# Two layers of a hybrid decoder, one step: masks, norms and state loads of the matrix-memory layer arranged in another way

## The chip, the cores and the metric

The kernel runs on one core of one Trainium2 chip. The metric is the device time of one execution in microseconds (us), from launch to end; the median of several runs is given. "The profiled execution" is one execution taken by the hardware profiler, and its span is the stretch from its first to its last recorded instruction. TensorE (PE) multiplies matrices, its weight loads (PEld) run beside it; VectorE (DVE), ScalarE (ACT) and GpSimd (POOL) work element by element; SyncE (SP) issues most of the transfers. PSUM is the memory that TensorE writes to; a bank of it is 512 float32 columns here.

## The reference

A trunk of two layers is applied to a prompt of 256 tokens and to 8 samples of 8 tokens each, 320 tokens of width 1024 in all, with the same weights. Layer 0 mixes tokens by a chunked spatial gate, layer 1 by a matrix memory (mLSTM) with 8 heads, keys of 128 and values of 256; a gated feed-forward layer with a short convolution follows each. The change touches the memory layer alone. Cut to what matters:

```python
p = rmsnorm(x, g) @ w_in                       # q, k, v, o and the gates i, f of 8 heads
qk = silu(causal_dwconv(p_qk, conv_buf, conv_w, conv_b))
# per head, in chunks, exact recurrence:
sc  = einsum('td,sd->ts', q, k) * exp(D - m_t)
num = w_inter * (q @ C) + sc @ v
den = w_inter * (q @ n) + sum(sc)
h   = num / max(|den|, exp(-m_t))
C_new = decay * C + (k * g).T @ v
n_new = decay * n + sum(k * g)
# group norm of each head's row, then the output gate
hn = (h - mean(h)) * rsqrt(var(h) + EPS) * gn_g
y  = (sigmoid(o) * hn) @ w_out
```

Returned are, beside the activations, the new states C, n and m for the prompt and for each of the 8 samples.

## The kernel before, in words

The activations lie transposed in SBUF, 8 tiles of 128 features by 320 tokens. Weights pass through once, in blocks of 128 by 1024 (`raw`, 4 buffers, loaded by SP's queue in a fixed order). Float32 accuracy is had from reduced-precision passes: each `raw` is cast to a high part `wh` by ScalarE (line 129), and VectorE subtracts to a low part `wl` (line 130); activations are split likewise (`xh`, `xl`). One block is 24 matmuls into a PSUM tile `pm`: high by high, high by low, low by high for each of 8 k-tiles (`chunk`, `block`). The order of TensorE's instructions is written out by hand and pinned; the order on VectorE, ScalarE, GpSimd and SP is made by a scheduler from data, buffers and the order of the source. PSUM tiles come from two pools, `psm` (3 banks, the blocks) and `psa` (5 banks, everything else); which of the 5 banks a tile gets is settled when the program is built, and a matmul then waits until that bank's last readers are through.

The memory layer, `layer_b`, lies at some 430 to 735 us of the profile.

`gates` comes first. A block `pg` gives the two gates of all heads. `norm_cols` then sums the squares of each token by matmuls against ones (three tiles of tokens, two passes each, into `pc`), and GpSimd raises the mean to the power -1/2 (`rc`, a token per partition). With `twice=True` the third tile is a copy `acc2` in which each sample token stands twice (line 210), because the sample rows of the values are kept doubled. The first q block `p0` follows on TensorE, then `norm_row` turns `rc` into a row for all partitions (`dg`, `pb`, `rb`). After that come the exponents and running maxima of the gates, five further blocks, and the transposes `pt` that give them per token (`colsT`). When `gates` ends, the pool of its rows closes and the pool `hb` opens.

Each head h then goes through two q and k blocks (`qk_epi`), two v blocks (`v_epi`), and two o blocks (`o_epi`), and between them, in TensorE's order:

- `scores`: the mask rows `pMb`, the scores `psc`, exponentials `w` by ScalarE, `Pf` = scores times `w`, split into `Ph` and `Pl`; the sample part goes to `Ps` in two disjoint halves, the first of which, `Pr`, is made by VectorE (line 690);
- `k_nat`: the keys transposed back (`pk`), scaled and split for the prompt (`kgh`, `kgl`), and for the samples `kz`, which is the key times one mask minus `kr`, the key times another (lines 721 and 722, VectorE);
- `finish(h - 1)`: the normalised rows `hn` transposed (`phn`), gated (`y_b`) and split (`yhb`, `ylb`, lines 839 and 840);
- `v_nat`: the values transposed back (`pv`), scaled by `rc` and split (`vh`, `vl`, lines 705 and 706);
- `hand_over`: 16 matmuls of the queries with the states C into `num` (`inter`), products `pcs` of keys and values of the samples, four tiles (`state_sample`), and the first two updates of C (`state_out`, line 762);
- in the next head `close` (the other two updates, the rest of the numerators, the prompt's state `pCp`) and `stats`: means and variances of the numerators (`mv`), the denominators `dn` and their maximum `rd`, the scale `sl` and the offset `nb`, and `hn` by ScalarE (line 801).

`state_in(h)` asks for the four states of a head (`C0`); head 0's is called after `gates`, because its tiles come from `hb`. Of the output weights, some blocks are worked early, in heads 4 to 6. The last head has a tail of its own. The first loop pass (h = 1) also holds the second half of head 0, so its order differs: `hand_over(0)` follows the first k block, `stats(0)` the second v block.

Of the kernel before, what the change touches and what calls it, by code (L numbers as in the profile page):

```python
# [10 lines left out]
F32 = mybir.dt.float32  # L11
F32R = mybir.dt.float32r
AF = mybir.ActivationFunctionType
# [3 lines left out]
P = 128  # L17
EPS = 1e-6
TP = 256
NB, NS = 8, 8  # L20
T = TP + NB * NS
D = 1024
# [3 lines left out]
NH = 8  # L26
# [11 lines left out]
class Net:  # L38
# [150 lines left out]
    @staticmethod  # L189
    def spread(x):  # L190

        return x.rearrange("p (g d s) -> p g d s", g=4, d=2)
# [8 lines left out]

    def norm_cols(self, parts=None, twice=False):

        nc = self.nc
        parts = parts or [self.acc]
        pc = self.psa.tile([P, 512], F32, tag="pa", name="pc")
        pv = pc[:, 0:6].rearrange("p (t e) -> p t e", e=2)
        if twice:
            acc2 = self.tp.tile([P, P], F32, tag="acc2", name="acc2", bufs=1)
            nc.vector.tensor_copy(self.spread(acc2), self.twice(self.acc[:, TP:]))  # L210
        for t in range(3):
            for i, a in enumerate(parts):
                a_t = acc2 if twice and t == 2 else self.tokens(a, t)
                self.mm(pv[:, t, :], a_t, self.ones[:, :2], i == 0, i == len(parts) - 1)
        rc = self.tp.tile([P, 3], F32, tag="rc", name="rc", bufs=2)
        ms = self.tp.tile([P, 3], F32, tag="ms", name="ms", bufs=2)
        nc.vector.tensor_scalar(ms, pv[:, :, 0], 1.0 / D, EPS, op0=MULT, op1=ADD)
        nc.gpsimd.tensor_tensor(rc, ms, self.mhalf.to_broadcast([P, 3]), op=ALU.pow)
        self.rc, self.rc_twice = rc, twice

    def norm_row(self):

        nc = self.nc
        dg = self.tp.tile([P, T], F32, tag="sq", name="dg", bufs=2)
        pb = self.psa.tile([P, 512], F32, tag="pa", name="pb")
        for t in range(2):
            nc.vector.tensor_scalar(dg[:, t * P:(t + 1) * P], self.ident, self.rc[:, t:t + 1], None, op0=MULT)
        if self.rc_twice:
            nc.vector.tensor_scalar(dg[:, TP:].rearrange("p (g s) -> p g s", g=4), self.spread(self.ident)[:, :, 0, :],
                                    self.rc[:, 2:3], None, op0=MULT)  # L230
        else:
            nc.vector.tensor_scalar(dg[:, TP:], self.ident[:, 64:], self.rc[:, 2:3], None, op0=MULT)
        self.mm(pb[:, :T], self.ones, dg, True, True)
        rb = self.tp.tile([P, T], F32, tag="rb", name="rb", bufs=1)
        nc.scalar.copy(rb, pb[:, :T])
        self.rb = rb
# [261 lines left out]
    def layer_b(self):  # L498
# [5 lines left out]
        with ExitStack() as ctx:  # L504
# [4 lines left out]
            nS = lp.tile([P, NH, NB], F32, name="nS")  # L509
            nP = lp.tile([P, NH], F32, name="nP")  # L510
            gnh = lp.tile([P, 16], F32, name="gnh")
            colsT = lp.tile([P, 3, 96], F32, name="cols")
            X = lp.tile([P, 392], F32R, name="X")
            sel = lp.tile([P, NH, P], F32R, name="sel")
            mk = lp.tile([P, NB + 5], F32, name="mk")
            mxb = lp.tile([P, 64], F32, name="mxb")
            gm = lp.tile([P, 4, NH], F32, name="gm")
            mo = lp.tile([8, 9], F32, name="mo")
            mkr = lp.tile([P, NB], F32R, name="mkr")
            pads = []  # L520
# [11 lines left out]
            def gates(rp):  # L532
# [34 lines left out]
                nc.vector.tensor_tensor(gr, pg[:64, :T], gr, op=ADD)  # L567
                self.norm_cols(twice=True)
                p0 = self.block(KD, self.x_rhs)
                self.norm_row()  # L570
                nc.vector.tensor_tensor(zi, gr[:40], self.rb[:40, :], op=MULT)
                qk_epi(0, 0, p0)
                nc.vector.tensor_scalar(zi, zi, bif[:, 0:1], None, op0=ADD)
                nc.vector.scalar_tensor_tensor(az, z, -1.0, z, op0=MULT, op1=MAX)
# [84 lines left out]
            def scores(h):  # L659
# [8 lines left out]
                mm(sc[:, 384:448], s["ks"], q[:, TP:T], True, True)  # L668
                dec = hp.tile([P, NB], F32, tag="dec", name="dec", bufs=2)
                nc.vector.tensor_copy(dec, pb[:, 384:392])  # L670
                Qd = Qz.rearrange("p (g i r) -> p g i r", g=4, i=2)[:, :, :, :NS]
# [8 lines left out]
                for o in (0, TP):  # L680
# [8 lines left out]

                nc.vector.tensor_scalar(Pr, Pf[:, 384:], mk[:, NB:NB + 1], None, op0=MULT)  # L690
                nc.vector.tensor_tensor(spread(Ps)[:, :, 0, :], Pf[:, 384:].rearrange("p (g s) -> p g s", g=4),
                                        Pr.bitcast(F32).rearrange("p (g s) -> p g s", g=4), op=SUB)
                s["P"] = (Ph, Pl, dec)

            def v_nat(h):
                s = S[h]
                pv = [self.psa.tile([P, 512], F32, tag="pa", name="pv") for _ in range(2)]
                dsts = [pv[t // 2][:, (t % 2) * DV:] for t in range(3)]
                for t in range(3):
                    for e in range(2):  # L700
                        self.tr(dsts[t][:, e * P:(e + 1) * P], s["vT"][e][:, t * P:(t + 1) * P], self.ident)
                for t in (2, 0, 1):
                    dst = dsts[t]
                    sc = self.rc[:, t:t + 1]
                    nc.scalar.activation(vh[:, t, :DV], dst[:, :DV], AF.Copy, scale=sc)
                    nc.vector.scalar_tensor_tensor(vl[:, t, :DV], dst[:, :DV], sc, vh[:, t, :DV].bitcast(F32), op0=MULT, op1=SUB)

            def k_nat(h):
# [6 lines left out]
                kgl = hp.tile([P, 2, P], F32R, tag="kgl", name="kgl", bufs=1)  # L715
                kr = hp.tile([P, 2, P], F32R, tag="kr", name="kr", bufs=1)
                kz = hp.tile([P, 2, P], F32R, tag="kz", name="kz", bufs=1)
                src = pk[:, 2 * P:3 * P]

                for i in range(2):  # L720
                    nc.vector.tensor_scalar(kr[:, i, :], src, gm[:, 2 + i, h:h + 1], None, op0=MULT)
                    nc.vector.scalar_tensor_tensor(kz[:, i, :], src, gm[:, i, h:h + 1], kr[:, i, :].bitcast(F32), op0=MULT, op1=SUB)
                for t in range(2):
# [6 lines left out]
            def state_in(h):  # L730
                S[h]["C"] = []
                for i in range(4):
                    C0 = hp.tile([P, 2, CW], F32, tag="C0", name="C0", bufs=8)
                    nc.sync.dma_start(C0, I["C0"][h, :, 2 * i:2 * i + 2, :])
                    S[h]["C"].append(C0)

# [43 lines left out]
            def stats(h):  # L780
# [8 lines left out]
                nc.vector.tensor_tensor(rd, dn, colsT[:, :, 64 + h], op=MAX)  # L789
                nc.vector.reciprocal(rd, rd)  # L790
                t1 = hp.tile([P, 3], F32, tag="t1", name="t1", bufs=1)
                nc.vector.tensor_tensor(t1, mv[:, :, 1], rd, op=MULT)
                nc.vector.tensor_tensor(t1, t1, rd, op=MULT)
                nc.vector.tensor_scalar(t1, t1, EPS, None, op0=ADD)
                sl = hp.tile([P, 3], F32, tag="sl", name="sl", bufs=1)
                nc.gpsimd.tensor_tensor(sl, t1, self.mhalf.to_broadcast([P, 3]), op=ALU.pow)
                nc.vector.tensor_tensor(sl, sl, rd, op=MULT)
                nb = hp.tile([P, 3], F32, tag="nb", name="nb", bufs=1)
# [4 lines left out]
            def state_prompt(h):  # L803
                s = S[h]
                kgh, kgl, kz = s["kg"]
                dec = s["P"][2]
                pc = self.psa.tile([P, 512], F32, tag="pa", name="pCp")
                for t in range(2):
                    mm3(pc[:, :CW], kgh[:, t, :], kgl[:, t, :], vh[:, t, :], vl[:, t, :], t == 0, t == 1)
                for i in range(2):  # L810
                    mm(pc[:, 264:272], kz[:, i, :], mkr, i == 0, i == 1)
                Cp = hp.tile([P, DV], F32, tag="Cp", name="Cp", bufs=1)
                nc.scalar.copy(Cp, pc[:, :DV])
                nc.sync.dma_start(O["Cp"][h], Cp)
                nc.scalar.copy(nP[:, h:h + 1], pc[:, DV:DV + 1])
                nc.vector.tensor_tensor(nS[:, h, :], n0[:, h, :], dec, op=MULT)
                nc.vector.tensor_tensor(nS[:, h, :], nS[:, h, :], pc[:, 264:272], op=ADD)

# [71 lines left out]

            state_in(0)
            scores(0)
# [60 lines left out]
            begin(2)  # L953
            nc.sync.dma_start(O["nP"], nP)
            nc.sync.dma_start(O["nS"], nS)
# [59 lines left out]
def _lay_out(i):  # L1015
# [56 lines left out]
    for h in range(NH):  # L1072
# [3 lines left out]
    tok = s // 32 * 16 + s % 16  # L1076
    low, odd = s // 16 % 2, s // 8 % 2
    a["blk"] = np.concatenate([tok[:, None] // NS == np.arange(NB)[None, :], np.stack(
        [low, 1 - odd, odd, (1 - odd) * low, odd * low], axis=1)], axis=1).astype(f)
    a["mxb"] = np.where((tok[:, None] // NS == q[None, :] // NS) & (tok[:, None] <= q[None, :]), f(-1e30), f(1e4))  # L1080
# [27 lines left out]
```

## Time and profile before

| what | value |
|---|---|
| time, median of 3 runs | 977.2 us (976.13, 977.2, 979.38) |
| the profiled execution: its time | 977.89 us |
| its span | 975.8 us |
| TensorE busy | 957.5 us |
| VectorE, ScalarE, GpSimd busy | 686.7, 484.6, 71.9 us |
| data moved | 154.73 MB, mean 159 GB/s |

A row of a timeline gives start and duration in us, the engine, the line of the code, the operation, output and inputs by the program's names, size, and how many instructions of the kind are taken together; in brackets stands how long the engine had been idle before, and after an arrow what ended that. A row of the waits gives for an engine's line who released it, then the sum, how often and the longest. A group's row gives busy time and the mean of one in ns. The clock is the share of full speed that TensorE was granted.

### The profile page before, as it was taken

Reading aid. Unit: us, or ns where it says so; the run is one execution under the profiler, and the core shown is the slowest. Engines: PE = TensorE matmul, PEld = TensorE weight load, DVE = VectorE, ACT = ScalarE, POOL = GpSimd, SP = SyncE. Lnnn points to the kernel's source line nnn. Section 1 sums busy time; section 2 is a strip of 40 time slices with the busy share of each in tenths; the row PEclk is TensorE's granted clock in tenths of the full one; section 3 lists DMA queues with packets and bytes.
Section 4 is the critical chain, followed back from the end, with each engine's and each line's share of the span. In section 5 each row is a group of like instructions: output and inputs, shape, how many; then the busy total and the mean of one; then the engine's idle time right before and its main releaser. Section 6 shows DMA issues by size and latency. Waiting matters only on the chain. (4 is left out here: it accounts for less than half of the span.)

```text
span 975.8 us, 17507 instructions
## 1 busy us (share of the span) xinstructions
PE 957.5 (98%) x6703; PEld 941.0 (96%) x6703; DVE 686.7 (70%) x1344; ACT 484.6 (50%) x846; POOL 71.9 (7%) x238
## 2 busy tenths in 40 slices
PE   9999999999999999999989999999999999999996
PEld 8999999999999999999889999999899999999996
DVE  6647985577777764548988887787787777775442
ACT  6437444445554543347456665464565455544332
POOL 0200000010000000012200110011001000000000
PEclk9999999999999999999999999999999999999999
DMA  8534434434444445553854556545273444444441
GB/s 283 193 119 159 140 133 155 152 133 149 151 152 151 148 147 152 150 190 101 279 188 156 189 174 221 170 160 164 73 239 137 152 152 151 152 146 149 147 129 54
DMA packets 55944, 154.73 MB, mean 159 GB/s; under 512 B 6758, under 2 KB 17638, under 8 KB 55862
## 3 DMA queue, kind: packets, MB, share of 16 engines
q1 hardware_dynamic: 55862, 153.62, 47.4%
q8 instruction: 53, 0.87, 0.4%
q14 instruction: 29, 0.24, 0.1%
HBM read 141.66 MB, written 11.94 MB: 157 GB/s over the span
## 5 line engine op out<-in xcount | busy, mean ns | idle before, releaser
L129 ACT CAST wh<-raw 128x1024 fp32r<-128x1024 f32 (+3 forms) x254 | 257.4, 1014 | 353.0 <-PE pm L47 221.9
L47 PE MATMUL pm<-xh,wh 128*128 128x320 f32 x1344 | 422.7, 315 | 1.2 <-ACT wh L129 1.2
L47 PE MATMUL pm<-xh,wl 128*128 128x320 f32 x1344 | 417.5, 311 | 0.1
L47 PE MATMUL pm<-xl,wh 128*128 128x320 f32 x1344 | 417.0, 310 | 0.0
L130 DVE TENSOR_TENSOR wl<-raw,wh 128x1024 fp32r<-128x1024 f32 (+3 forms) x254 | 300.2, 1182 | 124.5 <-ACT wh L129 122.4
L47 PEld LDWEIGHTS pm<-xh,wh 128*128 128x128 f32 x1344 | 253.9, 189 | 2.4 <-ACT wh L129 1.6
L47 PEld LDWEIGHTS pm<-xh,wl 128*128 128x128 f32 x1344 | 253.6, 189 | 0.7 <-DVE wl L130 0.7
L47 PEld LDWEIGHTS pm<-xl,wh 128*128 128x128 f32 x1344 | 253.9, 189 | 0.2
L47 PE MATMUL pm<-yh_f,wh 128*128 128x320 f32 x352 | 109.1, 310 | 0.0
L47 PE MATMUL pm<-yl_f,wh 128*128 128x320 f32 x352 | 108.6, 309 | 0.0
L47 PE MATMUL pm<-yh_f,wl 128*128 128x320 f32 x352 | 108.6, 309 | 0.0
L47 PEld LDWEIGHTS pm<-yl_f,wh 128*128 128x128 f32 x352 | 66.2, 188 | 0.0
L47 PEld LDWEIGHTS pm<-yh_f,wh 128*128 128x128 f32 x352 | 66.1, 188 | 0.0
L47 PEld LDWEIGHTS pm<-yh_f,wl 128*128 128x128 f32 x352 | 66.1, 188 | 0.0
L420 DVE SCALAR_TENSOR_TENSOR fcv<-fpad,vecs,fcv 128x336 f32<-128x336 f32 x88 | 49.6, 566 | 2.2 <-ACT fcv L418 0.7
L243 DVE TENSOR_TENSOR xT<-pm,xT 128x320 f32<-128x320 f32 x40 | 19.6, 491 | 41.6 <-PE pm L47 41.4
L47 PE MATMUL pm<-yhb,wh 128*128 128x320 f32 x128 | 40.3, 315 | 0.2 <-ACT yhb L839 0.2
L47 PE MATMUL pm<-ylb,wh 128*128 128x320 f32 x128 | 39.6, 310 | 0.4 <-DVE ylb L840 0.4
L47 PE MATMUL pm<-yhb,wl 128*128 128x320 f32 x128 | 39.5, 309 | 0.5 <-DVE wl L130 0.5
L47 PE MATMUL pm<-yh_a,wh 128*128 128x320 f32 x128 | 39.6, 309 | 0.0
L47 PE MATMUL pm<-yl_a,wh 128*128 128x320 f32 x128 | 39.5, 309 | 0.0
L47 PE MATMUL pm<-yh_a,wl 128*128 128x320 f32 x128 | 39.5, 309 | 0.0
(241 smaller groups left out, 1116.1 us busy)
## 6 DMA issues: line engine op xcount, KB each, us to landing
raw<-in_f_up SPq DMA_DIRECT2D x88, 512.0 KB, 3.2
raw<-in_b_win SPq DMA_DIRECT2D x48, 512.0 KB, 3.6
raw<-in_a_win SPq DMA_DIRECT2D x30, 512.0 KB, 3.2
raw<-in_f_dn SPq DMA_DIRECT2D x32, 448.0 KB, 3.3
C<-in_C SPq DMA_DIRECT2D x32, 258.0 KB, 5.3
raw<-in_a_wo SPq DMA_DIRECT2D x16, 512.0 KB, 3.7
raw<-in_f_dn SPq DMA_DIRECT2D x16, 512.0 KB, 3.4
out_Cs<-C SPq DMA_DIRECT2D x32, 256.0 KB, 3.9
```

Source lines behind the costliest of these rows:

```text
L47: self.pin(self.nc.tensor.matmul(out, lhsT, rhs, start=start, stop=stop))
L129: self.last_split = nc.scalar.copy(wh[:, :kn, :], raw[:, :kn, :])
L130: self.last_low = nc.vector.tensor_tensor(wl[:, :kn, :], raw[:, :kn, :], wh[:, :kn, :].bitcast(F32), op=SUB)
L243: self.nc.vector.tensor_tensor(x, ps[:, :T], x, op=ADD)
L420: nc.vector.scalar_tensor_tensor(cv, pd[:, i:i + NC], self.vec(w + i * KF), cv, op0=MULT, op1=ADD)
```

## The change

1. `norm_cols` sums the plain accumulator. The doubled copy is made by ScalarE in a new function `norm_twice`, called after `norm_row`; a matmul of its own (`pc2`) and a power of its own give `rc2`, which `v_nat` uses for the sample tile.
2. `state_in(0)` is called inside `gates`, after the first `qk_epi`; the `C0` tiles move to the layer's pool.
3. The first halves of `kz` and of the sample scores (`Pr`) are made by ScalarE with masks that carry a sign; VectorE adds the other half in one instruction each. `kr` goes.
4. The decay `dec` is copied by ScalarE and kept for all heads (`decs`); the ten columns of `pCp` with the normaliser are copied at once (`nPS`), and the samples' normaliser `nS` is made once, at the end, by two GpSimd instructions.
5. `stats` no longer divides by the denominator: variance plus EPS times its square goes to the power, which gives the scale directly.

```diff
+TINY = 1e-37
...
-                self.norm_cols(twice=True)
+                self.norm_cols()
                 p0 = self.block(KD, self.x_rhs)
                 self.norm_row()
+                self.norm_twice()
                 nc.vector.tensor_tensor(zi, gr[:40], self.rb[:40, :], op=MULT)
                 qk_epi(0, 0, p0)
+                state_in(0)
...
+    def norm_twice(self):
+        nc = self.nc
+        acc2 = self.tp.tile([P, P], F32, tag="acc2", name="acc2", bufs=1)
+        nc.scalar.copy(self.spread(acc2), self.twice(self.acc[:, TP:]))
+        pc = self.psa.tile([P, 512], F32, tag="pa", name="pc2")
+        self.mm(pc[:, 0:2], acc2, self.ones[:, :2], True, True)
+        ms = self.tp.tile([P, 1], F32, tag="ms2", name="ms2", bufs=1)
+        rc = self.tp.tile([P, 1], F32, tag="rc2", name="rc2", bufs=1)
+        nc.vector.tensor_scalar(ms, pc[:, 0:1], 1.0 / D, EPS, op0=MULT, op1=ADD)
+        nc.gpsimd.tensor_tensor(rc, ms, self.mhalf, op=ALU.pow)
+        self.rc2 = rc
...
-                dec = hp.tile([P, NB], F32, tag="dec", name="dec", bufs=2)
-                nc.vector.tensor_copy(dec, pb[:, 384:392])
+                dec = decs[:, h, :]
+                nc.scalar.copy(dec, pb[:, 384:392])
...
-                nc.vector.tensor_scalar(Pr, Pf[:, 384:], mk[:, NB:NB + 1], None, op0=MULT)
-                nc.vector.tensor_tensor(spread(Ps)[:, :, 0, :], Pf[:, 384:].rearrange("p (g s) -> p g s", g=4),
-                                        Pr.bitcast(F32).rearrange("p (g s) -> p g s", g=4), op=SUB)
+                nc.scalar.activation(Pr, Pf[:, 384:], AF.Copy, scale=mk[:, NB + 5:NB + 6])
+                nc.vector.scalar_tensor_tensor(spread(Ps)[:, :, 0, :], Pf[:, 384:].rearrange("p (g s) -> p g s", g=4),
+                                               mk[:, NB:NB + 1], Pr.bitcast(F32).rearrange("p (g s) -> p g s", g=4),
+                                               op0=MULT, op1=ADD)
...
-                    sc = self.rc[:, t:t + 1]
+                    sc = self.rc[:, t:t + 1] if t < 2 else self.rc2
...
-                    nc.vector.tensor_scalar(kr[:, i, :], src, gm[:, 2 + i, h:h + 1], None, op0=MULT)
-                    nc.vector.scalar_tensor_tensor(kz[:, i, :], src, gm[:, i, h:h + 1], kr[:, i, :].bitcast(F32), op0=MULT, op1=SUB)
+                    nc.scalar.activation(kz[:, i, :], src, AF.Copy, scale=gm[:, i, h:h + 1])
+                    nc.vector.scalar_tensor_tensor(kz[:, i, :], src, gm[:, 2 + i, h:h + 1], kz[:, i, :].bitcast(F32), op0=MULT, op1=ADD)
...
-                    C0 = hp.tile([P, 2, CW], F32, tag="C0", name="C0", bufs=8)
+                    C0 = lp.tile([P, 2, CW], F32, tag="C0", name="C0", bufs=8)
...
-                nc.vector.reciprocal(rd, rd)
-                t1 = hp.tile([P, 3], F32, tag="t1", name="t1", bufs=1)
-                nc.vector.tensor_tensor(t1, mv[:, :, 1], rd, op=MULT)
-                nc.vector.tensor_tensor(t1, t1, rd, op=MULT)
-                nc.vector.tensor_scalar(t1, t1, EPS, None, op0=ADD)
+                nc.vector.scalar_tensor_tensor(rd, rd, EPS, rd, op0=MULT, op1=MULT)
+                nc.vector.scalar_tensor_tensor(rd, rd, TINY, mv[:, :, 1], op0=MAX, op1=ADD)
                 sl = hp.tile([P, 3], F32, tag="sl", name="sl", bufs=1)
-                nc.gpsimd.tensor_tensor(sl, t1, self.mhalf.to_broadcast([P, 3]), op=ALU.pow)
-                nc.vector.tensor_tensor(sl, sl, rd, op=MULT)
+                nc.gpsimd.tensor_tensor(sl, rd, self.mhalf.to_broadcast([P, 3]), op=ALU.pow)
...
-                nc.scalar.copy(nP[:, h:h + 1], pc[:, DV:DV + 1])
-                nc.vector.tensor_tensor(nS[:, h, :], n0[:, h, :], dec, op=MULT)
-                nc.vector.tensor_tensor(nS[:, h, :], nS[:, h, :], pc[:, 264:272], op=ADD)
+                nc.scalar.copy(nPS[:, h, :], pc[:, DV:DV + 10])
...
-            state_in(0)
             scores(0)
...
-            nc.sync.dma_start(O["nP"], nP)
+            nc.gpsimd.tensor_tensor(nS, n0, decs, op=MULT)
+            nc.gpsimd.tensor_tensor(nS, nS, nPS[:, :, 2:], op=ADD)
+            nc.sync.dma_start(O["nP"], nPS[:, :, 0])
             nc.sync.dma_start(O["nS"], nS)
...
+    sign = 1 - 2 * low
     a["blk"] = np.concatenate([tok[:, None] // NS == np.arange(NB)[None, :], np.stack(
-        [low, 1 - odd, odd, (1 - odd) * low, odd * low], axis=1)], axis=1).astype(f)
+        [low, (1 - odd) * sign, odd * sign, (1 - odd) * low, odd * low, sign], axis=1)], axis=1).astype(f)
```

TensorE's order stays, but for the third column sum, which reads `acc`, and for `pc2` behind `pb`. On SP's queue the four loads of head 0's states come directly behind the last small table of `gates` (`mxb`) and ahead of three weight loads; those of head 1 are spread among the weight loads that follow.

More of the change, by code (lines that the diff above doesn't have):

```diff
@@ L200, in tokens, with norm_cols @@
         return a[:, (0, P, T - P)[t]:(P, TP, T)[t]]
-    def norm_cols(self, parts=None, twice=False):
+    def norm_cols(self, parts=None):
         nc = self.nc
@@ L207, in norm_cols @@
         pv = pc[:, 0:6].rearrange("p (t e) -> p t e", e=2)
-        if twice:
-            acc2 = self.tp.tile([P, P], F32, tag="acc2", name="acc2", bufs=1)
-            nc.vector.tensor_copy(self.spread(acc2), self.twice(self.acc[:, TP:]))
         for t in range(3):
             for i, a in enumerate(parts):
-                a_t = acc2 if twice and t == 2 else self.tokens(a, t)
-                self.mm(pv[:, t, :], a_t, self.ones[:, :2], i == 0, i == len(parts) - 1)
+                self.mm(pv[:, t, :], self.tokens(a, t), self.ones[:, :2], i == 0, i == len(parts) - 1)
         rc = self.tp.tile([P, 3], F32, tag="rc", name="rc", bufs=2)
@@ L218, in norm_cols @@
         nc.gpsimd.tensor_tensor(rc, ms, self.mhalf.to_broadcast([P, 3]), op=ALU.pow)
-        self.rc, self.rc_twice = rc, twice
+        self.rc = rc
+    def norm_twice(self):
[9 more added lines that the diff above has]
+        self.rc2 = rc
     def norm_row(self):
@@ L227, in norm_row @@
             nc.vector.tensor_scalar(dg[:, t * P:(t + 1) * P], self.ident, self.rc[:, t:t + 1], None, op0=MULT)
[L228 to L232, printed above, removed]
+        nc.vector.tensor_scalar(dg[:, TP:], self.ident[:, 64:], self.rc[:, 2:3], None, op0=MULT)
         self.mm(pb[:, :T], self.ones, dg, True, True)
@@ L509, in layer_b @@
             nS = lp.tile([P, NH, NB], F32, name="nS")
-            nP = lp.tile([P, NH], F32, name="nP")
             gnh = lp.tile([P, 16], F32, name="gnh")
@@ L514, in layer_b @@
             sel = lp.tile([P, NH, P], F32R, name="sel")
-            mk = lp.tile([P, NB + 5], F32, name="mk")
+            mk = lp.tile([P, NB + 6], F32, name="mk")
             mxb = lp.tile([P, 64], F32, name="mxb")
@@ L518, in layer_b @@
             mo = lp.tile([8, 9], F32, name="mo")
+            decs = lp.tile([P, NH, NB], F32, name="decs")
+            nPS = lp.tile([P, NH, 10], F32, name="nPS")
             mkr = lp.tile([P, NB], F32R, name="mkr")
@@ L715, in k_nat @@
                 kgl = hp.tile([P, 2, P], F32R, tag="kgl", name="kgl", bufs=1)
-                kr = hp.tile([P, 2, P], F32R, tag="kr", name="kr", bufs=1)
                 kz = hp.tile([P, 2, P], F32R, tag="kz", name="kz", bufs=1)
@@ L805, in state_prompt @@
                 kgh, kgl, kz = s["kg"]
-                dec = s["P"][2]
                 pc = self.psa.tile([P, 512], F32, tag="pa", name="pCp")
@@ L810, in state_prompt @@
                 for i in range(2):
-                    mm(pc[:, 264:272], kz[:, i, :], mkr, i == 0, i == 1)
+                    mm(pc[:, CW:CW + NB], kz[:, i, :], mkr, i == 0, i == 1)
                 Cp = hp.tile([P, DV], F32, tag="Cp", name="Cp", bufs=1)
```

## The prediction

> **What bounds the kernel now.** I read the page first, then the waits of TensorE's weight loads within the memory layer (430 to 735 us), then the timeline at each place that the change touches, and the table of windows for the granted clock. The page's head and the waits (us in total, times, longest):
>
> ```profile
> PE 957.5 (98%) x6703; PEld 941.0 (96%) x6703; DVE 686.7 (70%) x1344; ACT 484.6 (50%) x846; POOL 71.9 (7%) x238
> ...
> PEld psc L47 <- ACT kh L251: 2.6, 5, 0.8
> PEld pcs L47 <- DVE vl L706: 1.6, 1, 1.6
> PEld num L47 <- DMA C<-in_C: 1.5, 3, 0.5
> PEld pc L47 <- DVE acc L210: 1.3, 1, 1.3
> PEld pm L47 <- DVE ylb L840: 0.9, 2, 0.5
> ```
>
> TensorE is busy for 98% of the span. VectorE, at 70%, is relieved by the change, but that is worth nothing as such: only a TensorE wait that goes counts. The waits listed are small, and each has its own place, so the forecast is a sum of a few of them, a microsecond or two each. The profiled execution took 977.89 us, 0.7 above the median of the runs (977.2, of three that lie 3.25 apart); the sum goes against the former. A difference of 0.3%, 2.9 us, is about what a measurement of this kernel tells from no change.
>
> **Gates: the doubled column goes.** Before, the third column sum needs a copy of the doubled accumulator on VectorE (line 210), queued behind a 1.22 us weight split; TensorE stood, and its clock was halved right after.
>
> ```profile
> 433.37 0.61 PE L47 MATMUL pc<-ones,acc 128*128 128x2 f32 x4
> 435.22 0.58 PE L47 MATMUL pc<-ones,acc 128*128 128x2 f32 x2 [1.24 <-DVE acc L210]
> 435.67 0.61 PE L47 MATMUL pm<-xh,wh 128*128 128x320 f32 x1
> 438.72 0.31 PE L47 MATMUL pm<-xh,wl 128*128 128x320 f32 x1
> 484.92 0.31 PE L47 MATMUL pm<-xl,wh 128*128 128x320 f32 x1
> 488.14 0.31 PE L47 MATMUL pm<-xh,wl 128*128 128x320 f32 x1
> ...
> 431.85:435.26 3.41, 2.17 (x14) 1.00 0.66 179
> 435.26:438.68 3.42, 3.42 (x13) 0.50 0.84 271
> 483.05:486.46 3.41, 2.17 (x16) 1.00 1.00 324
> 486.46:489.88 3.42, 2.46 (x16) 1.00 0.66 254
> ```
>
> The window rows give its limits, its length, TensorE's busy time with its matmuls, the granted clock, and the DMA share with GB/s. Afterwards all six passes run through: at some 0.12 us each, estimated from the four in 0.61, the next block starts at 433.37 + 0.73 = 434.1 and not at 435.67, which is -1.57 (at least -1.24, the named wait). The block after it ran at clock 0.50: 11 intervals from 435.67 to 438.72 make 0.277 us each, against 22 from 484.92 to 488.14, 0.146 each. With the idle stretch gone I expect full clock, -11 x 0.131 = -1.43 (0 if it halves all the same). The doubled sum comes back as one fp32 matmul of two passes behind the row norm, +0.22 (up to 0.45, the 435.22 to 435.67 of the pair). Its copy is made by ScalarE long before. ScalarE, VectorE and GpSimd rows of the gates hang on that block's results and move forward with it. **Sum of the gates: -2.8** (-3.0 to -0.8).
>
> The four state loads of head 0 move ahead of three weight loads on SP's queue.
>
> ```profile
> C<-in_C SPq DMA_DIRECT2D x32, 258.0 KB, 5.3
> 433.76 1.27 SPq L114 DMA_DIRECT2D raw<-in_b_win  x2
> 451.24 2.00 ACT L129 CAST wh<-raw 128x1024 fp32r<-128x1024 f32 x2
> ```
>
> 1.03 MB at the 324 GB/s of the fullest window row are an estimated 3.2 us for the weights behind them, which are issued from 433.76 on and cast from 451.24 on: nothing. These 17 us are the cover, and a delay of 3.2 uses a fifth of it.
>
> **Head 1, its first half.** The state matmuls of head 0 wait for their loads; afterwards these lie ready.
>
> ```profile
> 469.08 2.97 PE L47 MATMUL num<-C,Qz 128*32 128x258 f32 x16 [0.86 <-DMA C<-in_C]
> 494.96 1.08 PE L47 MATMUL num<-C,Qz 128*32 128x258 f32 x16
> 469.64 0.34 DVE L727 SCALAR_TENSOR_TENSOR kgl<-pk,cols,kgh 128x128 fp32r<-128x128 f32 x1
> 472.65 0.41 PE L47 MATMUL pm<-xh,wh 128*128 128x320 f32 x1
> ```
>
> They can start at 469.08 - 0.86 = 468.2 and last 1.08, as at 494.96. But the four products behind them take PSUM banks, and by the order of instructions of the changed kernel the fourth gets the bank of the transposed keys, free only after the second low part of the keys (469.64 + 0.34 = 470.0). So the block resumes at about 470.6, not at 472.65: -2.0. The update of the states that follows on VectorE costs back some 0.3 (0 to 0.6, half of a split), an estimate. Everything to the scores of head 1 comes 1.7 earlier.
>
> **Head 1, its second half.** Here a wait takes another's place. Call the start of the mask matmul T0.
>
> ```profile
> 482.06 0.34 PE L47 MATMUL pMb<-X,sel 128*128 128x392 f32 x1
> 482.81 0.33 PE L47 MATMUL psc<-qs,ks 128*128 128x64 f32 x2
> 484.39 0.44 PE L50 MATMUL pk<-ident,qs 128*128 128x128 f32 x2 [1.24 <-ACT w L678]
> 489.29 0.79 PE L50 MATMUL phn<-ident,hn 128*128 128x128 f32 x2 [0.84 <-ACT hn L801]
> 491.27 0.39 PE L47 MATMUL pm<-xh,wh 128*128 128x320 f32 x1
> 482.15 1.05 ACT L129 CAST wh<-raw 128x1024 fp32r<-128x1024 f32 x1 [0.95 <-PE pm L47]
> 484.11 1.22 DVE L130 TENSOR_TENSOR wl<-raw,wh 128x1024 fp32r<-128x1024 f32 x1
> 487.11 1.12 POOL L796 TENSOR_TENSOR sl<-t,mhalf 128x3 f32<-128x3 f32 x1 [1.38 <-DVE t L794]
> L801 ACT ACTIVATE hn<-num,nb,sl 128x256 f32<-128x256 f32 x24 | 11.8, 562 | 8.4 <-DVE nb L799 8.4
> ```
>
> Before, the transposes of the keys start at T0 + 2.33, when the exponentials have released a bank. In the changed order their bank is one of the numerators' of head 0, so they wait for that head's last normalised rows (hn). These come so: weight cast 1.05, denominators and their maximum 0.3, weight split 1.22, the two small steps 0.4, the power on GpSimd 1.12, its product 0.2, one hn 0.56, together T0 + 4.9 with the hops between. The group norm from undivided sums shortens this chain by a reciprocal, two products and an addition, but it now stands in front of TensorE, which is idle from T0 + 1.1 (482.81 + 0.33) to T0 + 4.9: 3.8 us. In return the transposes of hn wait no more (before 0.84 at the first, and paced by hn through the next). The block after them starts, estimated, at T0 + 10.1, before at 491.27 - 482.06 = 9.21: +0.9. **Head 1 nets -0.8** (-2 to +1).
>
> **The clock there.** An idle stretch of 1.24 us in a window with 2.17 busy was followed by a halved one; windows of head 1 with the same 2.17, and with 2.46, were not. So the threshold lies about there, and 3.8 us, wherever the limits of the windows fall, leave one window with at least 1.9 idle. I expect one halved window more: **+1.5** (0 to 2.5), about the 1.43 of the gates. [...]
>
> **Heads 2 to 6.** VectorE loses some nine small instructions a head; ScalarE gains two products of the keys (the shape of kgh, 0.364 each), the high part of the scores (the shape of L679, 0.284) and a small copy, some 1.2 us. Where does this meet TensorE?
>
> ```profile
> L726 ACT ACTIVATE kgh<-pk,cols 128x128 fp32r<-128x128 f32 x16 | 5.8, 364 | 5.5 <-DVE kz L722 3.3 <-PE pm L47 2.2
> L679 ACT ACTIVATE w<-w 128x64 f32<-128x64 f32 x8 | 2.3, 284 | 0.0
> ...
> 513.30 0.16 DVE L799 SCALAR_TENSOR_TENSOR nb<-mv,sl 128x3 f32<-128x3 f32 x1
> 515.70 0.37 PE L47 MATMUL psc<-qh,khl 128*128 128x256 f32 x1
> 524.40 0.48 ACT L705 ACTIVATE vh<-pv,rc 128x256 fp32r<-128x256 f32 x1
> 525.41 0.48 DVE L706 SCALAR_TENSOR_TENSOR vl<-pv,rc,vh 128x256 fp32r<-128x256 f32 x1
> 526.07 0.39 PE L47 MATMUL pcs<-vh,kz 32*128 32x256 f32 x4
> ```
>
> Ahead of the scores, nb, which comes an estimated 2.4 us earlier behind its shorter chain, puts hn ahead of the gate's tanh and the cast of the keys, and the weight split ahead of the low keys: followed through the new order, these reach the score matmul at about 515.77 against 515.70. Ahead of the fourth product (526.07), the value's high part ended at 524.88 and its low part could only start at 525.41, so 0.5 of ScalarE's added work is covered; the rest falls before that, where ScalarE had idle time. I take **+0.3** for all five heads, between -2 (the 2.6 us of waits for the keys gone) and +3.
>
> **Last head and end.** The output blocks wait twice, 0.9 us in all, for a low part that VectorE made late.
>
> ```profile
> 693.02 0.41 PE L47 MATMUL pm<-ylb,wh 128*128 128x320 f32 x1 [0.26 <-DVE ylb L840]
> ```
>
> It comes earlier in the new order: **-0.6** (0 to -1.4). The sums of the normaliser move to GpSimd, twice 64 columns once instead of 16 small VectorE steps, and their output goes out 4 bytes at a time; both end long before the following feed-forward layer does, so nothing, unless the packets hold up its weights (up to +0.6).
>
> **The sum.** -2.8 - 0.8 + 1.5 + 0.3 - 0.6 = -2.4: 975.5 by the profiled execution, 974.8 from the median; I take 975.1.
>
> **The rivals.** (A) The new wait in head 1 is there but halves nothing, as the rows from 483.05 and 486.46 allow, whose windows were idle by a third and followed by full clock: 1.5 less, 973.6. [...] (B) The change doesn't bring the early states: the block in head 1 still resumes at about 472.6, because the low keys and not the loads end the wait. Against it stand the loads' own 1.5 us of waits; for it, that VectorE's row at 469.64 is the last thing before. Then 1.7 is lost: 976.8. (C) Slower: ScalarE's 1.2 us a head fall on the path. The point from which this decides is a high value later by more than 0.5 us; if all 1.2 arrive there, each fourth product of five heads is late by about 0.65, and head 1's, which already waits 1.6 for the low value, by 1.2: +4.4, 979.5, and with one more halved window 980.9. Against it: ScalarE is busy for half the span, and some of the new work takes VectorE's place earlier in the same chain.
>
> **How the numbers follow.** Forecast 0.50 (own range 973.4 to 976.8), A 0.24, B 0.10, C 0.16. Faster by over 0.3% (under 974.3): a third of the forecast and two thirds of A, 0.33. Slower by over 0.3% (above 980.1): half of C and a little of the unknown at the end, 0.10. The rest, 0.57, lies within. The range goes from 972.4 (A with the heads' better end) to 979.6 (the middle of C), which leaves a tenth on either side.
>
> **What would show it.** Right: the window from 435.26 at full clock; the state matmuls of head 0 with no DMA wait; the first transposes of the keys in head 1 waiting for hn, nearly 4 us, with a clock of 0.5 in the window after; heads 2 to 6 within 0.2 us each of their old length. Wrong: a product in heads 2 to 6 that waits for the low value (C), a block in head 1 that resumes at its old distance (B), or no halved clock there (A).

## The result, and the profile after

The changed kernel takes 975.63 us (median of 20 runs, 972.82 to 978.5), the kernel before 977.16 us beside it (median of 20): ratio 0.9982, interval 0.9975 to 0.999. That is 1.5 us less, within the 0.3% that the forecast called the likeliest outcome, and 0.5 us from the forecast of 975.1. The profiled execution of after took 975.54 us. The page's head of after:

```profile
span 973.8 us, 17461 instructions
PE 955.2 (98%) x6705; PEld 941.2 (97%) x6705; DVE 679.1 (70%) x1272; ACT 490.7 (50%) x879; POOL 75.1 (8%) x241
```

VectorE's 7.6 us less are not what moved the time. The waits of the weight loads between 430 and 735 us show what did:

```profile
PEld pk L51 <- ACT hn L806: 3.8, 1, 3.8
PEld psc L48 <- DVE khl L258: 3.5, 5, 0.7
...
PEld pcs L48 <- DVE vl L716: 1.6, 1, 1.6
...
PEld pcs L48 <- DVE kgl L736: 0.6, 1, 0.6
...
PEld pm L48 <- DVE ylb L842: 0.2, 1, 0.2
```

The waits for the doubled column, for the states' loads, for `kh` and for the exponentials are gone from the list; a wait of 3.8 us for `hn` is new, and the scores now wait for the keys' low part `khl`. The timeline of after, in the gates and in head 1:

```profile
432.57 0.83 PE L48 MATMUL pc<-ones,acc 128*128 128x2 f32 x6
433.26 0.39 PE L48 MATMUL pm<-xh,wh 128*128 128x320 f32 x1
...
464.59 1.08 PE L48 MATMUL num<-C,Qz 128*32 128x258 f32 x16
466.08 0.34 DVE L736 SCALAR_TENSOR_TENSOR kgl<-pk,cols,kgh 128x128 fp32r<-128x128 f32 x1
466.48 0.38 PE L48 MATMUL pcs<-vh,kz 32*128 32x256 f32 x1 [0.37 <-DVE kgl L736]
467.14 0.41 PE L48 MATMUL pm<-xh,wh 128*128 128x320 f32 x1
...
476.91 0.34 PE L48 MATMUL pMb<-X,sel 128*128 128x392 f32 x1
477.66 0.33 PE L48 MATMUL psc<-qs,ks 128*128 128x64 f32 x2
480.99 1.47 ACT L806 ACTIVATE hn<-num,nb,sl 128x256 f32<-128x256 f32 x3 [0.47 <-DVE nb L804]
481.61 0.69 PE L51 MATMUL pk<-ident,qs 128*128 128x128 f32 x2 [3.62 <-ACT hn L806]
488.21 0.38 PE L51 MATMUL phn<-ident,hn 128*128 128x128 f32 x2
489.44 0.39 PE L48 MATMUL pm<-xh,wh 128*128 128x320 f32 x1
```

All six column sums run through; the state matmuls take 1.08 us at once; the fourth sample product waits for the second `kgl`; and the transposes `pk` start 4.70 us behind the mask rows, with TensorE idle since 477.99 (477.66 + 0.33). In the traces of before and after the stretches at half clock within the memory layer last 3.42 and 6.83 us; a stretch of 3.41 us, half of the latter, is called a window here. The limits of the rows at full clock are counted from those at half clock in such steps; in before the 423.25 us between its two halved windows (12.01 to 435.26) are 124 of them. The clock in head 1, in the table of windows of after:

```profile
477.36:480.77 3.41, 0.63 (x7) 1.00 0.94 355
480.77:484.18 3.41, 2.57 (x11) 0.50 0.86 290
484.18:487.60 3.42, 3.42 (x14) 0.50 0.01 2
```

Since TensorE's order is nearly the same in both kernels, the same matmul can be laid beside itself. Start times (us), after minus before, and the step since the row above:

| matmul | before | after | difference | step |
|---|---|---|---|---|
| first column sum of the gates | 433.37 | 432.57 | -0.80 | |
| second matmul of the block behind `p0` | 441.31 | 437.77 | -3.54 | -2.74 gates |
| mask rows of head 1 | 482.06 | 476.91 | -5.15 | -1.61 head 1, first half |
| block behind the transposes of head 1 | 491.27 | 489.44 | -1.83 | +3.32 head 1, second half |
| third score product of head 6 | 646.96 | 646.14 | -0.82 | +1.01 heads 2 to 6 |
| last instruction | | | -1.95 | -1.13 last head |

The first 0.80 us are not the change's, which begins with the memory layer: 0.72 of them are there by 12 us, where the profile of before has a window at half clock (8.60 to 12.01, clock 0.50) and that of after has none (clock 1.00 up to 20 us). Between the executions compared below such differences of the start are up to 1.7 us. So of the 1.95 us between the two profiles 1.15 belong to the change.

### The profile page after: what moved, and what is told of

It reads as the page before. It is cut to its first block, busy times and chain, and to the rows that moved or that the text cites. A ratio compares the mean times of both kernels' runs of the same rounds, so it can differ in the third digit from the quotient of the medians.

```text
span 973.8 us, 17461 instructions
## 1 busy us (share of the span) xinstructions
PE 955.2 (98%) x6705; PEld 941.2 (97%) x6705; DVE 679.1 (70%) x1272; ACT 490.7 (50%) x879; POOL 75.1 (8%) x241
## 4 chain that ended last, share of the span: by engine, by line
PE 84%; issue 10%; DVE 3%; ACT 1%; DMA 1%; SPq 0%; POOL 0%; DVEq 0%; POOLq 0%; ACTq 0%
PE pm L48 77%; PE num L48 2%; PE pmix L48 1%; DVE wl L131 1%; PE pCp L48 1%; PE pcs L48 1%; PE pvt L51 1%; DMA xT<-in_xT 1%; ACT wh L130 0%; PE psc L48 0%; PE pv L51 0%; PE phn L51 0%; PE pk L51 0%; PE pc L48 0%; PE pg L48 0%
```

## The experiments

Theory: the change wins in the gates and in head 1, and loses much of it to one new wait, for `hn`, with a clock that falls behind it; the wait comes from the bank that `pk` gets. Rivals: it is VectorE's relief that counts; or the early states bring the wait. Each median stands beside runs of the kernel before on the same chip (977.3, 977.5 and 977.8 us in the three groups, against 977.16 beside the changed kernel; so medians of different groups compare to within some 0.6 us); "at the same matmuls" means differences as in the table above, from behind the start.

**One part alone on the kernel before.** e1 is the plain column sums with `norm_twice`, e2 the early states, e3 the new formula in `stats`:

```diff
e1:
+                self.norm_cols()
                 p0 = self.block(KD, self.x_rhs)
                 self.norm_row()
+                self.norm_twice()
...
e2:
                 qk_epi(0, 0, p0)
+                state_in(0)
...
e3:
...
+                nc.vector.scalar_tensor_tensor(rd, rd, EPS, rd, op0=MULT, op1=MULT)
+                nc.vector.scalar_tensor_tensor(rd, rd, TINY, mv[:, :, 1], op0=MAX, op1=ADD)
```

> The kernel before with part 1 alone (plain column sums, doubled copy by ScalarE with a matmul of its own). Theory (the sum's gates term is its own and nothing hangs on the rest): the wait of 1.24 us at the column sums and the halved window behind it go, one small matmul comes, 2.6 to 2.8 us less from the first block of the gates to the end: 974.4 against 977.2. Rival 1 (the clock halves in the gates all the same): only 1.3 less, 975.9. Rival 2 (the gates run ahead of the state loads, which are still issued after them): the head's state matmuls wait as much longer as was won, 976.5 or more.

Measured 974.99 us, ratio 0.9977 (0.9967 to 0.9988). At the same matmuls 2.7 us are won in the gates and kept to the end. The median alone doesn't part the theory (974.4) from the first rival (975.9), both of which lie in the interval; the profile does, since its gates ran at full clock (1.00) throughout. The second rival fell. So the theory holds for the profiled execution.

> The kernel before with part 2 alone (states of head 0 asked for in the gates, tiles in the layer's pool). Theory: the state matmuls of head 0 no longer wait for their loads, the keys' low part is next, and the rest comes 1.7 us earlier; the transposes of the keys in head 1 still wait for the exponentials as before, so all of it reaches the end: 975.5. Rival (the loads were not what decided, the keys' low part comes at the same time): 977 and the block in head 1 at its old distance behind the state matmuls.

Measured 975.96 us, ratio 0.9984 (0.9972 to 0.9996). The state matmuls no longer wait, and at the fourth sample product 1.9 us are won; but 0.9 go again at the prompt's state, where the updates of C on VectorE are late:

```profile
473.84 0.47 DVE L763 SCALAR_TENSOR_TENSOR C<-C,dec,pcs 128x256 f32<-128x256 f32 x1
474.46 0.36 PE L47 MATMUL pCp<-vh,kgh 128*128 128x258 f32 x1 [0.74 <-DVE C L763]
```

So 0.9 reaches the end and not 1.7; in the changed kernel this place costs 0.3. That VectorE's relief by part 3 makes the difference is not shown: in e12 below, where VectorE has that work again, the wait is 0.3 too. In the profiled execution of e2 the gates still wait for the doubled column, yet no window there is halved:

```profile
430.46:433.88 3.42, 2.93 (x19) 1.00 0.71 224
433.88:437.29 3.41, 2.65 (x18) 1.00 0.90 248
```

Before, the idle stretch lay wholly in one window; here its limits fall into the middle of it. By these two profiles the 1.4 us of the clock in the gates are won in some executions and not in others. The granted clock says the same beyond them: one window at half clock takes an estimated 0.0018 off the mean of an execution (half of 3.41 in 975.8 us), and 11 of the 47 executions of the kernel before beside these experiments had 0.998 (975.8 to 976.8 us), where the profiled one, with two such windows, had 0.994.

> The kernel before with part 5 alone (group norm from undivided sums). In its built order the transposes of the keys in head 1 still take the bank of the mask rows, so no wait for hn. Theory: the normalised rows come about 1 us earlier in each head, which takes away most of the waits for hn in head 1 (1.1 us) and some of the waits for the keys ahead of the scores in heads 2 to 6 (2.6 us in all): 974.5 to 976. Rival (VectorE's chain was hidden and other work queued on the engines decides): within 0.5 of 977.2.

Measured 972.43 us, ratio 0.995 (0.9935 to 0.9965): more than the theory, and the largest of the three. The profiled execution is the slowest of the six (974.61 us, with the gates' window at half clock as before); at the same matmuls it wins 3.7 us. 1.0 us goes at the first transposes of `hn` in head 1, and between 0.4 and 0.8 in each of heads 2 to 6, where the scores no longer wait for the keys:

```profile
514.19 0.30 ACT L252 CAST kh<-qs 128x128 fp32r<-128x128 f32 x1
514.52 0.29 DVE L253 TENSOR_TENSOR khl<-qs,kh 128x128 fp32r<-128x128 f32 x1 [0.49 <-ACT kh L252]
514.81 0.28 PE L48 MATMUL psc<-qhl,kh 128*128 128x256 f32 x1
514.93 0.32 PE L48 MATMUL psc<-qh,khl 128*128 128x256 f32 x1
```

**The changed kernel with one thing undone.** e4 has the old `stats`; its `pk` gets the bank of the mask rows, as before, and so waits for the exponentials that read them.

> The changed kernel with part 5 undone (divided sums again). By its built order the transposes of the keys in head 1 then wait for the exponentials, not for hn. Theory (the new formula is what moved the bank, and with it brought the 3.8 us wait and the halved clock): the wait is about 1.3 us, the block behind it runs at full clock, head 1 is some 3.5 us shorter than in the changed kernel, heads 2 to 6 lose up to 1: 972 to 973.5. Rival (wait and halved clock come from the states' earlier arrival, not from the formula): 975.6 or more, with the halved block still there.

Measured 970.64 us, ratio 0.9928 (0.9913 to 0.9944): 5 us faster than the whole change, more than was expected. The waits and windows of e4:

```profile
PEld pk L51 <- ACT w L687: 3.0, 1, 3.0
```

```profile
478.23:481.64 3.41, 1.18 (x10) 1.00 0.93 280
481.64:485.05 3.41, 2.81 (x11) 0.50 1.01 375
...
479.64 1.22 DVE L131 TENSOR_TENSOR wl<-raw,wh 128x1024 fp32r<-128x1024 f32 x1
481.06 0.28 DVE L685 SCALAR_TENSOR_TENSOR w<-pMb,cols,mxb 128x64 f32<-128x64 f32 x1
481.45 0.73 ACT L687 ACTIVATE w<-pMb,cols 128x256 f32<-128x256 f32 x2 [1.43 <-DVE t L802]
```

The wait for `hn` is gone, but `pk` still waits 3.0, not 1.3, for the exponentials. These start behind VectorE's row of sample masks (line 685), which stands behind a weight split; the trace names the step after it (line 802), but of the two only line 685 writes a tile that the exponentials use. One window is halved, where none was expected, so head 1 is 2.2 us shorter than in the changed kernel and not 3.5. The expectation was wrong on the heads too: they don't lose, they win another 3.3 us against the changed kernel, some 0.65 each. In e3 (the formula alone) and e2 (the early states alone) `pk` waits for the exponentials as well. So the wait for `hn` takes the formula together with another part; which one, no run tells. Here `khl` is made at 512.29, ahead of VectorE's next weight split; in the changed kernel it stands behind it:

```profile
512.60 1.23 DVE L131 TENSOR_TENSOR wl<-raw,wh 128x1024 fp32r<-128x1024 f32 x1 [0.81 <-ACT wh L130]
512.63 0.33 ACT L257 CAST kh<-qs 128x128 fp32r<-128x128 f32 x1
513.74 0.28 DVE L258 TENSOR_TENSOR khl<-qs,kh 128x128 fp32r<-128x128 f32 x1
514.08 0.39 PE L48 MATMUL psc<-qh,khl 128*128 128x256 f32 x1 [0.51 <-DVE khl L258]
```

**The idle stretch of head 1: filled, or used.** e5 puts idle work there, e6 moves the transposes of the keys behind the next block; e7 changes the order of the score products; e8 is e6 and e7.

```diff
e5:
+                if h == 1:
+                    for _ in range(14):
+                        mm(sc[:, 448:512], s["ks"], q[:, TP:T], True, True)
e6:
-                k_nat(h)
                 if h > 1:
+                    k_nat(h)
                     finish(h - 1)
...
                     o_epi(h, 0, blk())
                 if h == 1:
+                    k_nat(h)
                     finish(0)
e7:
-                mm3(sc[:, :TP], kh, kl, qh, ql, True, True)
                 mm(sc[:, TP:384], k[:, P:TP], q[:, P:TP], True, True)
                 mm(sc[:, 384:448], s["ks"], q[:, TP:T], True, True)
+                mm3(sc[:, :TP], kh, kl, qh, ql, True, True)
```

> The changed kernel with 14 more small fp32 matmuls in head 1 between the scores and the transposes of the keys, written to columns that nobody reads; they fill some 3 of the 3.8 us in which TensorE waits. Theory (the idle stretch halves the clock): the block behind runs at 0.146 us a matmul instead of 0.267, the wait for hn ends at the same time, 2.7 us less: 972.9. Rival (the halved clock there comes from elsewhere, or the short matmuls don't count as work): the block is halved as before, 975.6 to 976.

Measured 974.28 us, ratio 0.9965 (0.9952 to 0.9979). In the profiled execution both windows ran at full clock, and at the same matmuls 2.7 us are won behind the wait, with the wait for `hn` ending when it did:

```profile
477.30:480.70 3.40, 3.40 (x30) 1.00 0.62 194
480.70:484.10 3.40, 2.91 (x25) 1.00 1.02 356
```

So here the half clock comes with the idle stretch: 0.50 in after, 1.00 where the stretch is filled. From the two profiles alone the phase of the windows would stay a rival, since they lie 1.4 us otherwise against the mask rows here than in after. The medians differ by less, 1.35 us, but the mean clock of all executions goes the same way: 0.996 or more in six of the nine here, in two of the 20 of the changed kernel.

> The changed kernel with the transposes of the keys in head 1 moved behind the next block of 24 matmuls in TensorE's order. Theory: the block (3.5 us) runs in the time in which TensorE waited for hn, at full clock; 0.3 to 0.5 of the wait stay, 6 us less in head 1, of which up to 1 returns where values and keys are late for the samples' products: 970 to 971. Rival (hn only moves back with the block, since its engines take the block's weights first): 973 or more.

Measured 969.86 us, ratio 0.9921 (0.9906 to 0.9936). As the theory has it: at the same matmuls the block comes to be 6.8 us ahead, 0.9 return at the transposes of `hn`, and 5.9 reach the end. By the medians this alone is worth nearly four times the whole change. What is left of the wait for `hn`:

```profile
PEld pk L51 <- ACT hn L806: 0.3, 1, 0.3
```

> The changed kernel with the two plain score products put ahead of the three split ones in each head. Theory: the low part of the keys, for which the third split product waits 0.6 us in heads 2 to 6, is then covered by 0.3 to 0.5 of other work a head: 1.5 to 2.5 us less in all, 973.4. Rival (the split products now wait for the keys ahead of them, the plain ones for their copy): no gain, 975.6.

Measured 973.97 us, ratio 0.9954 (0.9937 to 0.9971). Heads 2 to 6 win 1.9 us at the same matmuls, 0.4 each; the rest of their wait stays. This run shows the clock from another side. Its stretch in head 1 is as long as in the changed kernel (3.8), but the limits of the windows fall into the middle of it, and nothing is halved:

```profile
476.24:479.65 3.41, 1.64 (x13) 1.00 0.92 249
479.65:483.06 3.41, 1.61 (x12) 1.00 0.98 349
```

Of its seven executions two took 970.5 and 970.8 us (the profiled one among them) with a mean clock of 0.998, the others 973.6 to 975.1 with 0.992 to 0.994. So some 2.7 of the profiled execution's gain are the clock's, and only the 1.9 in the heads are the new order's.

> e6 and e7 together. Theory: the two places are apart, so the gains add: 968 to 969.5. Rival: the heads' later waits (values for the samples' products) take back what the scores win: as e6, 970 to 971.

Measured 967.86 us, ratio 0.9898 (0.9882 to 0.9915). The gains add: e8 is 2.0 us below e6, as e7 is 1.7 below the changed kernel.

**What the formula costs, and what part 3 brings.** e9 is e4 with the move of e6; e10 has e7's order too; e12 is e4 with the first halves of keys and scores on VectorE again; e11 tries to hold VectorE to make `khl` before the weights.

> e4 (divided sums, the rest as changed) with the transposes of the keys in head 1 behind the next block, as in e6. Theory (head 1's stall and the later heads' wait are two separate effects of the formula): e4's remaining wait of 3.1 us in head 1 and its one halved window (1.4) are covered by the block, the heads stay as in e4: 970.6 - 4 = 966.6, below e6 by the 3.3 us that the heads lose to the formula. Rival (hn, later by the division, now stops the block's successor): 968.5 or more.

Measured 966.74 us, ratio 0.9888 (0.9874 to 0.9903), the best with e10. Both effects of the formula are separate, as expected. What waits are left in e9:

```profile
PEld phn L51 <- ACT hn L810: 1.0, 2, 0.6
PEld pm L48 <- DVE wl L131: 0.8, 1, 0.8
PEld pcs L48 <- DVE vl L716: 0.7, 1, 0.7
PEld pcs L48 <- DVE kgl L736: 0.6, 1, 0.6
```

> e9 with the plain score products first, as in e7. Theory (e7 gains only where the low keys are late, and in e4 they are not): within 0.5 of e9, 966.6. Rival (the order of the products is worth something by itself): 965 or less; or the plain products wait for the doubled keys: 967.5 or more.

Measured 966.71 us, ratio 0.9887 (0.987 to 0.9905): no more than e9. The order of the score products is worth something only where `khl` is late.

> e4 with the first halves of keys and sample scores on VectorE again (part 3 undone as to the engine; the masks stay). Theory (what e4's heads win over the kernel before, 2.4 us in heads 2 to 6 and 1.2 in the last, comes from VectorE's relief by part 3): that goes, 970.6 + 3.6 = 974.2. Rival (it comes from the decay and normaliser steps of part 4, or from the order alone): 970.6 to 971.5.

Measured 972.1 us, ratio 0.9945 (0.9932 to 0.9958): 1.5 above e4, between theory and rival. At the same matmuls the last head loses 1.5 us, where it waits for the high part of its outputs (1.2 in one wait), heads 2 to 6 lose 1.1 and the first half of head 1 some 0.5; against that 1.7 come back in head 1, where the samples' products waited for `vl`. The wait of the last head in e12:

```profile
PEld pm L48 <- ACT yhb L845: 1.2, 1, 1.2
```

So part 3, beside the old formula, brings what the last head wins, and its gain elsewhere (1.6) is paid again in head 1: VectorE's relief is worth 1.5 us there, less than the gates or the wait for `hn`. Part 4 was not taken out by itself.

```diff
e11:
+            with ExitStack() as es:
+                if getattr(self, "key_low", None) is not None:
+                    es.enter_context(self.tc.issue_after(self.key_low.ins))
...
+                self.last_low = nc.vector.tensor_tensor(wl[:, :kn, :], raw[:, :kn, :], wh[:, :kn, :].bitcast(F32), op=SUB)
```

> The changed kernel with VectorE held to make the low keys of heads 2 to 7 before the two next low parts of weights. Theory (the low keys are late in heads 2 to 6 only because a weight split of 1.22 us stands ahead of them): the waits of 0.6 to 0.7 us before the third score product go, 3.3 us less, head 1 as in the changed kernel: 972.3. Rival (the weights' low parts are then what is late): blocks wait for them, 975 or more.

Measured 1013.9 us, ratio 1.0369 (1.035 to 1.0389). The first of the two splits that were held back is the one that the running block needs, so that block stood for 3.4 us in each of heads 2 to 6 and for 2.5 in the last, and in all six the clock was 0.50 in the window after. In head 2:

```profile
514.16 0.64 PE L48 MATMUL pm<-xh,wl 128*128 128x320 f32 x1 [3.39 <-DVE wl L138]
```

The scores no longer wait for `khl` in it, but the run doesn't tell what the right order would bring. That `khl` is late because of the split ahead of it rests on e3 and e4, where it goes first and the wait is gone.

## Why the prediction was right, point by point

- **Gates**: -2.8 forecast, -2.74 in the profiles and -2.7 in e1. The clock's half of it was read from one profile of the kernel before; in the profile of e2, where the limits of the windows fall otherwise, the same wait is followed by a clock of 1.00.
- **Head 1, first half**: -1.7 forecast, -1.61. The chain was the one named: loads ready, then the bank of `pk` behind the second `kgl`. The 0.3 for the updates of C is right in the changed kernel; with the early states alone it is 0.9 (e2).
- **Head 1, second half**: the new wait was forecast from T0 + 1.1 to T0 + 4.9 and came from 1.1 to 4.7. The block after the transposes came 12.53 behind T0 (489.44 - 476.91), where T0 + 10.1 and one halved window, 11.6 in all, were forecast. The term that was mis-sized is the clock: +1.5 for one window, where the profile has two in a row, whose block ran at 0.267 us a matmul, against 0.146, for 22 of them: 2.7 us. Filling the stretch takes exactly that away (e5). Without the clock the block would have come at 9.9, close to the 10.1.
- **The clock's condition**: rival A happens, in two of seven executions of e7, and by its clock in one of the 20 of the changed kernel (972.82 us at a mean of 0.997; the profiled one, with two halved windows, has 0.994). The prediction had a stretch of 3.8 us halve a window "wherever the limits of the windows fall"; in e7 they fell so that both windows stayed idle for 1.8 us, and the clock behind each was 1.00. So in these two traces it goes with where the limits fall (477.36 in after, 476.24 in e7). Windows with 0.63 us busy (after) and 1.18 (e4) were followed by a clock of 0.50, those with 1.64 and 1.61 (e7) by 1.00.
- **Heads 2 to 6**: +0.3 forecast, +1.01. The place was right, the step to the score matmul (515.77 against 515.70, 0.07 a head) was too small, for it came to 0.20 on the mean: the low keys start only after the split ends, and the third product waits 0.5 to 0.7. What was not seen is that the same parts in another combination win 2.3 and 2.7 us there against the kernel before (e4, e3).
- **Last head**: -0.6 forecast, -1.13; the wait for the high part went too.
- **Rival B** fell: the early states did bring the block forward. **Rival C** fell: no product of heads 2 to 6 waits longer for the low value.
- **The sum**: -2.4 forecast against -1.15 in the profiles behind the start and -1.5 in the medians. Head 1 came out 0.9 dearer than its terms, heads 2 to 6 0.7 dearer, the last head 0.5 cheaper. That the forecast came so near to the measured time is in part luck, since these errors have both signs.

## What to carry to other kernels

A shorter chain is not a faster kernel: the formula that won most by itself cost about 5 us beside the other parts, because with them the order on VectorE and ScalarE and the choice of a PSUM bank came out differently; after such a change look at who waits for each bank, not at the instructions saved. Where TensorE, whose order is pinned here, has a gap that can't be closed, put its next independent block into it: moving three transposes behind a block won 5.8 us, nearly four times the change. When executions differ by the granted clock (a mean of 0.992 to 0.998 in those of e7), compare the same instruction in two traces and not only medians.

## What was not expected of the hardware

The halved clock cost nearly twice what was put down for it (2.7 against 1.5), since two windows in a row ran at 0.50. The first of them was itself partly idle (2.57 busy); a window at 0.50 with 2.81 busy, in e4, was followed by full clock. Whether that idle time brings the second is not shown.

TensorE's busy time in a window does not by itself tell whether the next is halved. In the gates of the kernel before, 2.17 us busy were followed by 0.50, in its head 1 the same 2.17 were not; and in head 1 of e11 2.04 were followed by 0.50, in that of after 2.04 were not:

```profile
492.67:496.08 3.41, 2.04 (x33) 1.00 0.34 106
496.08:499.50 3.42, 3.42 (x14) 0.50 0.80 293
...
494.42:497.83 3.41, 2.04 (x25) 1.00 0.39 119
497.83:501.24 3.41, 3.41 (x26) 1.00 0.76 267
```

The first two rows are of e11, the others of after. Some 0.65 us of the gates' window were column sums, matmuls of two columns; the window of e11 has none of them, and all but one of its matmuls are the narrow ones of `num` and `pcs` (128*32 and 32*128). What decides, and whether there is a threshold at all, stays open.
